# Three row norms of a two-layer kernel: transposed unscaled row by row into one kept tile, scaled and split there

## The chip, the cores and the metric

The kernel is one program on one core of a Trainium2 chip. The metric is the device time of one execution in microseconds. The kernel before was run three times: 2165.43, 2167.75 and 2170.39 us, median 2167.75.

## The reference, cut to what matters

512 tokens of width 1024 go through two transformer layers and a final norm; all data are float32. Every block starts from a row norm, `y = x * rsqrt(mean(x*x) + eps) * gain`, with one factor per token (row) and one gain per column.

```python
# layer 1
h = rms_norm(x, norm_mix);  proj = h @ w_in          # 1024 -> 5632
x = x + (gated mix of a recurrent branch and a differential attention) @ w_out
x = x + hier_moe(rms_norm(x, norm_moe), ...)         # 32 experts, two per token
# layer 2
z = rmsnorm(h, norm_mix_2) @ w_in_2
h = h + (gated mix of an RWKV-7 branch and a sparse attention) @ w_out_2
h = h + cross_attention(rmsnorm(h, norm_cross), rmsnorm(mem, norm_mem), ...)
h = h + hier_moe_2(rmsnorm(h, norm_ffn), ...)
out = rmsnorm(h, norm_final)
```

## The kernel before

The running sum `acc` (128 partitions, four row tiles t of 128 tokens, 1024 columns) stays in SBUF for the whole program. The stages follow one another: `dense1` (layer 1 up to its output projection), `moe` (experts), `dense2` (layer 2 up to its output projection), `cross` (cross attention), `moe` again, `final`. 

**Dense products.** `dense_steps` multiplies normed activations held transposed (`hT`, eight slices k of 128 channels by 512 tokens) with weights. Each operand is held as a high and a low half and a product is three matmuls (`mm3`). For each k a weight slice of 128x512 is split by ACT (`wh`, line 194) and DVE (`wl`, line 195) into three buffers; the split stands in a block of its own with high priority.

**The norm that feeds them** is what the change is about. It stands at three places: at the start of `dense1` (norm_mix), at the start of `dense2` (norm_mix_2) and at the start of `cross` (norm_cross_2). It has three steps. (1) The squares of the rows are summed, in halves of 512 columns as the output projection or the last expert block finishes them (`half_square`, lines 273 to 275; at the start `_norm_tile`, whole rows, row tile by row tile), and `row_scale` (lines 281 to 287) turns them into the four columns of `r`, one factor per token. (2) `_norm4` (lines 289 to 297) multiplies the rows by `r`, three row tiles on DVE and one on ACT, into a tile of 16 KB per partition. (3) `_norm_tp` (lines 299 to 309) turns the scaled rows with 32 transposes on PE into eight PSUM banks, and ACT (line 307, times the gain) and DVE (line 308) split each bank into `hT`'s halves.

**Between the first expert stage and `dense2`** stands a loop (`extra`, line 1075) for expert rows beyond the fixed blocks. It makes no turn with these inputs, but all engines meet at it. The weights of `dense2` are loaded by SP after it.

**Order of the work.** A list scheduler orders each engine's queue from a simulated time line and from priorities: the order of the program, or, inside a block of high priority, a count that starts again at the start of the program. Where `self.pinned` is set (the expert stage), PE's order is the program's. A pool of tiles that is opened over memory of closed pools waits until these are no longer used.

**Weight slots.** Weights of the expert stages come in pieces of 1 MB on SP's queue, in a fixed cycle of slots (`rings`, `plan`, `ahead`, `wslot`): two slots x, seven y, three z, and two m of pool `ringm`, which `moe` opens (line 879). SP issues them in order, each when its slot is free. The same queue loads the weights of `cross`, which go into the slots x and y.

```python
for t, x in enumerate(xs):                               # _norm_tp, lines 303 to 309
    for k, b in enumerate(banks):
        nc.tensor.transpose(b[:, t * 128:(t + 1) * 128], x[:, k * 128:(k + 1) * 128], self.c("ident"))
for k, b in enumerate(banks):
    nc.scalar.activation(hi[:, k, :w], b[:, :w], AF.Copy, scale=gain[:, k:k + 1])
    nc.vector.scalar_tensor_tensor(lo[:, k, :w], b[:, :w], gain[:, k:k + 1], hi[:, k, :w].bitcast(F32),
                                   op0=ALU.mult, op1=ALU.subtract)
```

Of the kernel before, what the change touches and what calls it, by code (L numbers as in the profile page):

```python
# [24 lines left out]
F32 = mybir.dt.float32  # L25
# [4 lines left out]
AF = mybir.ActivationFunctionType  # L30
# [5 lines left out]
D = 1024  # L36
# [141 lines left out]
class Net:  # L178
    def __init__(self, tc, ins, out, at, dump=None):
        self.tc, self.nc, self.I, self.out, self.at = tc, tc.nc, ins, out, at  # L180
        self.dump = dump or {}
        self.es = ExitStack()
        self.pinned, self.late, self.moe_pool = False, None, None
        self.todo, self.ready, self.cur, self.rest, self.bufs = [], [], [], [], {}
        self.banks("a0", "a1", "a2", "a3")
# [33 lines left out]
    def persistent(self):  # L219
        tc, nc, es = self.tc, self.nc, self.es  # L220
        self.P = es.enter_context(tc.tile_pool(name="persist", bufs=1))
        self.ps = es.enter_context(tc.tile_pool(name="ps", bufs=1, space=PSUM))
        P = self.P
        self.acc = P.tile([128, 4, D], F32, name="acc")
        n = sum(v[1] for v in self.at["consts"].values())
        self.cst = P.tile([128, n], F32, name="cst")
        self.dram = es.enter_context(tc.tile_pool(name="dram", bufs=1, space=bass.MemoryType.DRAM))
        self.eps = P.tile([128, 1], F32, name="eps")
        nc.vector.memset(self.eps, 1e-6)
        self.nq = P.tile([128, 3, 4], F32, name="nq")  # L230
        self.r = P.tile([128, 4], F32, name="r")

    def c(self, name):
# [38 lines left out]

    def half_square(self, t, i, junk, vector=False):

        self._square(vector, junk, self.acc[:, t, i * 512:(i + 1) * 512], self.nq[:, i, t:t + 1])

# [11 lines left out]

    def _norm4(self, outs):

        with self.tc.high_priority():
            for t in range(4):
                r = self.r[:, t:t + 1]
                if t == 1:
                    self.nc.scalar.activation(outs[t], self.acc[:, t, :], AF.Copy, scale=r)
                else:
                    self.nc.vector.tensor_scalar(outs[t], self.acc[:, t, :], r, None, op0=ALU.mult)

    def _norm_tp(self, xs, gain, hi, lo):
        nc = self.nc  # L300
        w = len(xs) * 128
        banks = [self.bank(c + str(i)) for c in "da" for i in range(4)]
        for t, x in enumerate(xs):
            for k, b in enumerate(banks):
                nc.tensor.transpose(b[:, t * 128:(t + 1) * 128], x[:, k * 128:(k + 1) * 128], self.c("ident"))
        for k, b in enumerate(banks):
            nc.scalar.activation(hi[:, k, :w], b[:, :w], AF.Copy, scale=gain[:, k:k + 1])
            nc.vector.scalar_tensor_tensor(lo[:, k, :w], b[:, :w], gain[:, k:k + 1], hi[:, k, :w].bitcast(F32),  # L308
                                           op0=ALU.mult, op1=ALU.subtract)

# [22 lines left out]
    def wslot(self, src, pool, tag="wslot", n=None):  # L333

        k = src.shape[1] // 512
        t = pool.tile([128, k, 512], F32, name="wslot", tag=tag, bufs=self.bufs.get((pool, tag)))
# [14 lines left out]
    def ahead(self, n):  # L351
        while self.todo and len(self.ready) < n:
            pool, tag = next(self.where)
            pool = {"late": self.late, "moe": self.moe_pool}.get(pool, pool)
# [61 lines left out]
    def dense1(self, rings, late):  # L416
# [285 lines left out]
        def gate(i):  # L702
            gt[i] = big("gt%d" % i)
            dense(8, hT, "T", lambda j, b: nc.scalar.activation(gt[i][:, j, :], b, AF.Tanh, scale=0.5))
# [168 lines left out]
    def moe(self, W, ring, after=None):  # L873
# [4 lines left out]
        L = es.enter_context(tc.tile_pool(name="moe", bufs=1))  # L878
        self.moe_pool = es.enter_context(tc.tile_pool(name="ringm", bufs=NM))
        acc, cm, br, rs, lps, gain = self.acc, self.cm, self.br, self.rs, self.lps, self.gain  # L880
# [189 lines left out]
        def extra():  # L1070
# [4 lines left out]
            with tc.For_i(0, n):  # L1075
# [28 lines left out]
                for _ in scatter(scat(sid), y, square):  # L1104
                    pass
                self.row_scale()

# [67 lines left out]
        for p in range(16):  # L1175
# [54 lines left out]
        for _ in steps:  # L1230
            pass
        self.pinned = False
        self.row_scale()
# [8 lines left out]
    def dense2(self):  # L1242
# [67 lines left out]
        AR = self.acc.rearrange("p t n -> p (t n)").rearrange("p (q c s n) -> p q c s n", q=4, c=8, s=2)  # L1310
        BK = big("X2", (128, 4, 8, 2, 64))
        v4 = lambda t: t.rearrange("p (c t) -> p c t", t=64)
# [184 lines left out]

        Zs = big("X2", (128, 2, 4, 8, 64))
        Zt, Z = Zs[:, 0], Zs[:, 1]
# [236 lines left out]
        for i in range(2):  # L1736
# [5 lines left out]
            if i == 0:  # L1742
                self.sqrt_table()
        self.row_scale()
        es.close()


    def cross(self, rings, late):
# [13 lines left out]
        hT = [A.tile([128, 8, 512], F32R, name="hT0"), B.tile([128, 8, 512], F32R, name="hT1")]  # L1762
        xn = [x[:, t, :] for x in (B.tile([128, 2, D], F32, name="xn%d" % i, tag="q%d" % i) for i in range(2)) for t in range(2)]
        self._norm4(xn)
        self._norm_tp(xn, col("norm_cross_2"), hT[0], hT[1])
        oT = []
# [73 lines left out]
def net(tc, I, out, at, dump=None):  # L1840
# [3 lines left out]
    def rings(es, n, table, name, first):  # L1844
# [6 lines left out]
        k = len(first)  # L1851
        z, yy, xg, m = ("late", "wslot"), ("late", "yy"), ("late", "xg"), ("moe", "wslot")
        seq = [x] * 2 + [y] * NRING
# [54 lines left out]
```

## Time and profile before

| what | value |
|---|---|
| median of three runs | 2167.75 us (2165.43 to 2170.39) |
| profiled execution, its own time | 2170.49 us |
| its span in the trace | 2168.5 us |
| PE busy | 2079.4 us, 96% of the span |
| first products of `dense1`, `dense2`, `cross` | at 13.66, 1002.35 and 1522.34 us |
| mean granted clock of TensorE | 0.98 of full speed |

Times in the trace are microseconds from the start of the span. A matmul's end is modelled, so PE's busy share says where PE has work, not how fast it goes. Waits are put down to the event that came last.

### The profile page before, as it was taken

Reading aid. Unit: us, or ns where it says so; the run is one execution under the profiler, and the core shown is the slowest. Engines: PE = TensorE matmul, PEld = TensorE weight load, DVE = VectorE, ACT = ScalarE, POOL = GpSimd, SP = SyncE. Lnnn points to the kernel's source line nnn. Section 1 sums busy time; section 2 is a strip of 40 time slices with the busy share of each in tenths; the row PEclk is TensorE's granted clock in tenths of the full one; section 3 lists DMA queues with packets and bytes.
Section 4 is the critical chain, followed back from the end, with each engine's and each line's share of the span. In section 5 each row is a group of like instructions: output and inputs, shape, how many; then the busy total and the mean of one; then the engine's idle time right before and its main releaser. Section 6 shows DMA issues by size and latency. Waiting matters only on the chain. (4 is left out here: it accounts for less than half of the span.)

```text
span 2168.5 us, 29754 instructions
## 1 busy us (share of the span) xinstructions
PE 2079.4 (96%) x11910; PEld 1348.1 (62%) x11914; DVE 986.8 (46%) x2014; ACT 676.4 (31%) x1313; POOL 162.5 (7%) x140
## 2 busy tenths in 40 slices
PE   8999998999999999998988999999998999999996
PEld 6777786785544444546666776767777554444443
DVE  4674344652432333325477474454454332333334
ACT  5364433453111111115434333444444111111112
POOL 0420001200000000000332100011010000000000
PEclk9999999999999999999988999999999999999998
DMA  4222212667999999973122112113532999999994
GB/s 178 87 77 70 75 62 78 247 236 310 412 418 420 419 419 419 419 311 117 61 76 76 40 64 83 54 57 112 228 136 100 375 415 419 420 419 420 419 419 161
DMA packets 96319, 505.87 MB, mean 233 GB/s; under 512 B 21089, under 2 KB 26209, under 8 KB 44465
## 3 DMA queue, kind: packets, MB, share of 16 engines
q1 hardware_dynamic: 90992, 490.09, 56.9%
q10 hardware_dynamic: 4688, 11.66, 1.5%
q0 software_dynamic: 496, 2.17, 0.3%
q8 instruction: 96, 1.57, 0.3%
q14 instruction: 47, 0.38, 0.0%
HBM read 494.83 MB, written 8.91 MB: 232 GB/s over the span
## 5 line engine op out<-in xcount | busy, mean ns | idle before, releaser
L209 PE MATMUL ps_d<-wslot,xg 128*64 128x512 f32 x2048 | 446.4, 592 | 0.0
L209 PE MATMUL ps_d<-hT,wh 128*128 128x512 f32 x1056 | 344.2, 410 | 2.8 <-DVE hT L308 2.8
L209 PEld LDWEIGHTS ps_d<-wslot,xg 128*64 128x64 f32 x2048 | 148.3, 137 | 286.5 <-issue 277.1
L195 DVE TENSOR_TENSOR wl<-wslot,wh 128x512 fp32r<-128x512 f32 x236 | 169.4, 722 | 256.9 <-ACT wh L194 211.0
L194 ACT ACTIVATE wh<-wslot 128x512 fp32r<-128x512 f32 x260 | 163.2, 631 | 310.0 <-PE ps_d L209 239.8
L209 PEld LDWEIGHTS ps_d<-hT,wh 128*128 128x128 f32 x1056 | 197.5, 193 | 54.4 <-issue 9.3
L1023 DVE TENSOR_TENSOR s<-ps_d,s 128x512 f32<-128x512 f32 x32 | 22.1, 692 | 423.0 <-PE ps_d L209 423.0
L209 PE MATMUL ps_d<-hT,wl 128*128 128x512 f32 x528 | 205.7, 402 | 0.0
L209 PE MATMUL ps_a<-wslot,hidT 128*64 128x512 f32 (+1 forms) x832 | 178.3, 578 | 1.7 <-ACT hidT L1031 1.4
L209 PE MATMUL ps_d<-wh,hT 128*128 128x512 f32 x512 | 163.8, 397 | 3.1 <-ACT wh L194 1.4
L1061 DVE TENSOR_TENSOR acc<-acc,ps_a 128x512 f32<-128x512 f32 (+1 forms) x214 | 131.2, 664 | 54.9 <-PE ps_a L209 54.7
L209 PEld LDWEIGHTS ps_a<-wslot,hidT 128*64 128x64 f32 x832 | 58.7, 137 | 108.9 <-issue 100.4
L209 PE MATMUL ps_a<-yy,S 128*128 128x512 f32 (+1 forms) x428 | 114.6, 400 | 5.6 <-DVE acc L1061 5.6
L209 PEld LDWEIGHTS ps_d<-hT,wl 128*128 128x128 f32 x528 | 101.3, 192 | 24.0 <-issue 1.5
L209 PEld LDWEIGHTS ps_d<-wh,hT 128*128 128x128 f32 x512 | 95.6, 188 | 26.9 <-ACT wh L194 1.8
L998 ACT ACTIVATE xg<-ps_a,gain 128x256 f32<-128x256 f32 x102 | 48.2, 475 | 200.0 <-PE ps_a L209 200.0
L209 PE MATMUL ps_a<-oh,xs 128*128 128x256 f32 x816 | 107.1, 285 | 1.4 <-DVE oh L1150 1.4
L209 PEld LDWEIGHTS ps_a<-oh,xs 128*128 128x128 f32 x816 | 100.9, 191 | 9.6 <-issue 9.6
L1049 ACT ACTIVATE yy<-ps_a,gc 128x512 fp32r<-128x512 f32 (+1 forms) x52 | 34.9, 671 | 223.6 <-PE ps_a L209 192.2
L209 PE MATMUL ps_d<-wl,hT 128*128 128x512 f32 x256 | 101.3, 396 | 1.8 <-DVE wl L195 1.8
L209 PEld LDWEIGHTS ps_a<-yy,S 128*128 128x128 f32 x428 | 74.8, 188 | 31.4 <-DVE acc L1061 13.5
L1022 ACT ACTIVATE s<-ps_d 128x512 f32<-128x512 f32 x32 | 19.1, 598 | 199.3 <-PE ps_d L209 199.3
(586 smaller groups left out, 2798.8 us busy)
## 6 DMA issues: line engine op xcount, KB each, us to landing
wslot<-in_wm_dram SPq DMA_DIRECT2D x380, 1024.0 KB, 12.2
wslot<-in_wd_dram SPq DMA_DIRECT2D x108, 512.0 KB, 3.4
wslot<-in_wd_dram SPq DMA_DIRECT2D x19, 1024.0 KB, 15.2
wslot<-in_wm_dram SPq DMA_DIRECT2D x8, 512.0 KB, 14.4
C<-in_x_dram SPq DMA_DIRECT2D x4, 512.0 KB, 5.2
acc<-in_x_dram ACTq DMA_DIRECT2D x4, 512.0 KB, 5.5
kvd<-kvs ACTq DMA_DIRECT2D x8, 256.0 KB, 4.0
xd<-acc ACTq DMA_DIRECT2D x1, 2048.0 KB, 11.1
```

Of the source, the lines that this page charges most:

```text
L194: self.nc.scalar.activation(hi, src, AF.Copy)
L195: (lo_eng or self.nc.vector).tensor_sub(lo, src, hi.bitcast(F32))
L209: self.pin(self.nc.tensor.matmul(*a, **k))
L998: nc.scalar.activation(xg[:, k, :n], b[:, :n], AF.Copy, scale=gain[:, k:k + 1])
L1022: nc.scalar.activation(s1, hb[0], AF.Silu)
L1023: nc.vector.tensor_mul(s1, hb[1], s1)
L1049: nc.scalar.activation(y[0][:, c], b, AF.Copy, scale=gcol)
L1061: nc.vector.tensor_add(acc[:, t, c], acc[:, t, c], b)
```

## The change

The scaling moves behind the transposing. A tile `xt` (8 slices of 128 channels by 512 tokens, 16 KB per partition) is kept for the whole program. As soon as a half row tile of `acc` is final, `turn` transposes its four blocks unscaled into one PSUM bank and copies the bank into `xt`. When `r` is there, `normed` spreads it over partitions with four transposes into one PSUM bank, and for each of the eight slices DVE multiplies `xt` by the gain and by that bank, and `split` (ACT a copy, DVE a subtraction) makes the halves of `hT`. `_norm4` and `_norm_tp` are gone.

At the start of the program the norm by row tiles (`_norm_tile`) gives way to half squares and `turn`s of the loaded rows with one `row_scale` for all. After the first expert stage and in the output projection of `dense2` the `turn`s stand behind the additions to `acc`. The loop's body gets eight `turn`s as well. Squares and copies are divided between ACT and DVE.

`xt` also takes over other tiles: the two slots m (pool `ringm` is gone), the gates `gt0` and `gt1` of `dense1`, and `X2` of `dense2`. The memory reserved at the bottom of SBUF for descriptors of POOL's DMAs goes from its default of 16384 bytes per partition to 4096.

```diff
-    def half_square(self, t, i, junk, vector=False):
-        self._square(vector, junk, self.acc[:, t, i * 512:(i + 1) * 512], self.nq[:, i, t:t + 1])
+    def half_square(self, t, i, junk, vector=False, src=None):
+        src = self.acc[:, t, :] if src is None else src
+        self._square(vector, junk, src[:, i * 512:(i + 1) * 512], self.nq[:, i, t:t + 1])
...
-    def _norm4(self, outs):
-    def _norm_tp(self, xs, gain, hi, lo):
...
+    def turn(self, t, i, tag="a", vector=False, src=None):
+        src = self.acc[:, t, :] if src is None else src
+        b = self.bank(tag, (128, 4, 128))
+        for k in range(4):
+            c = i * 512 + k * 128
+            self.pin(self.nc.tensor.transpose(b[:, k, :], src[:, c:c + 128], self.c("ident")))
+        o = self.xt[:, 4 * i:4 * i + 4, t * 128:(t + 1) * 128]
+        if vector:
+            self.nc.vector.tensor_copy(o, b)
+        else:
+            self.nc.scalar.activation(o, b, AF.Copy)
+
+    def normed(self, gain, hi, lo):
+        nc = self.nc
+        b = self.bank("a")
+        with self.tc.high_priority():
+            for t in range(4):
+                nc.tensor.transpose(b[:, t * 128:(t + 1) * 128], self.r[:, t:t + 1].to_broadcast([128, 128]), self.c("ident"))
+            for k in range(8):
+                x = self.xt[:, k, :]
+                nc.vector.scalar_tensor_tensor(x, x, gain[:, k:k + 1], b, op0=ALU.mult, op1=ALU.mult)
+                self.split(hi[:, k, :], lo[:, k, :], x)
...  wslot
+        if pool == "xt":
+            t = self.xt[:, 4 * self.nxt:4 * self.nxt + 4, :]
+            self.nxt = 1 - self.nxt
...  dense1
-        with tc.high_priority():
-            for t in range(4):
-                self._norm_tile(xin[:, t, :], xin[:, t, :], wk, junk=self.acc[:, t, :])
-        self._norm_tp([xin[:, t, :] for t in range(4)], col("norm_mix"), hT[0], hT[1])
+        for t in range(4):
+            for i in range(2):
+                self.half_square(t, i, self.acc[:, t, i * 512:i * 512 + 512], t % 2, xin[:, t, :])
+                self.turn(t, i, "da"[i] + str(t), t % 2 == 0, xin[:, t, :])
+        self.row_scale()
+        self.normed(col("norm_mix"), hT[0], hT[1])
...  moe, last block of the first stage, behind the addition and square(t, c)
+                    if c.start == 512 and not after:
+                        self.turn(t, 0, "d%d" % (t % 3))
...  moe, behind the last scatter
+        if not after:
+            for t in range(4):
+                self.turn(t, 1, "d%d" % ((t + 1) % 3), t % 2 == 0)
         self.pinned = False
         self.row_scale()
         extra()
...  dense2
-        xn = big("X2", (128, 4, D))
-        self._norm4([xn[:, t, :] for t in range(4)])
-        self._norm_tp([xn[:, t, :] for t in range(4)], col("norm_mix_2"), hT[0], hT[1])
+        self.normed(col("norm_mix_2"), hT[0], hT[1])
...  dense2, output projection, i = 0 and 1
             dense(8, mx, "N", ev_o)
             if i == 0:
                 self.sqrt_table()
+            for t in range(4):
+                self.turn(t, i, vector=i and t % 2)
         self.row_scale()
...  cross
-        self._norm4(xn)
-        self._norm_tp(xn, col("norm_cross_2"), hT[0], hT[1])
+        self.normed(col("norm_cross_2"), hT[0], hT[1])
...  kernel
-    nc = _bacc.Bacc("TRN2", target_bir_lowering=False, num_devices=1)
+    nc = _bacc.Bacc("TRN2", target_bir_lowering=False, num_devices=1, dynamic_dma_scratch_size=4096)
```

## Rows read from the trace of the kernel before

**Rows 1.** The page's part 1: busy us (share of span) xinstructions.

```profile
PE 2079.4 (96%) x11910; PEld 1348.1 (62%) x11914; DVE 986.8 (46%) x2014; ACT 676.4 (31%) x1313; POOL 162.5 (7%) x140
```

**Rows 2.** Waits of PE, whole span: us in total, times, longest.

```profile
PE ps_d L305 <- DVE X L297: 9.7, 1, 9.7
...
PE ps_d L305 <- DVE C L264: 7.1, 1, 7.1
...
PE ps_d L305 <- DVE xn L297: 3.6, 1, 3.6
```

**Rows 3.** Windows, second expert stage; last columns: clock, DMA share, GB/s.

```profile
1740.00:1760.00 20.00, 20.00 (x112) 11.99 (x110) 7.19 (x14) 3.56 (x7) 0.00 (x0) 1.00 1.02 421
```

**Rows 4.** Timeline, start of program: start, us, instructions [idle before, releaser].

```profile
4.58 1.06 ACT L271 ACTIVATE acc<-C 128x1024 f32<-128x1024 f32 x1 [1.40 <-DMA C<-in_x_dram]
...
11.27 0.60 PE L305 MATMUL ps_d<-cst,C 128*128 128x128 f32 x4
...
11.71 0.60 PE L305 MATMUL ps_a<-cst,C 128*128 128x128 f32 x4
...
13.66 0.51 PE L209 MATMUL ps_d<-wh,hT 128*128 128x512 f32 x1 [1.36 <-DVE hT L308]
```

**Rows 5.** Timeline, from the first expert stage to dense2.

```profile
988.51 0.69 DVE L269 SCALAR_TENSOR_TENSOR sq<-acc 128x512 f32<-128x512 f32 x1 [1.36 <-ACT sq L271]
...
989.77 0.18 DVE L287 RECIPROCAL r<-nq 128x4 f32<-128x4 f32 x1 [0.36 <-ACT nq L286]
...
991.65 1.15 ACT L295 ACTIVATE X<-acc,r 128x1024 f32<-128x1024 f32 x1 [1.91 <-DVEq L1075]
...
991.94 25.77 SPq L338 DMA_DIRECT2D wslot<-in_wd_dram  x6
...
995.74 1.12 PE L305 MATMUL ps_d<-cst,X 128*128 128x128 f32 x4 [9.70 <-DVE X L297]
...
995.98 0.63 ACT L194 ACTIVATE wh<-wslot 128x512 fp32r<-128x512 f32 x1 [3.18 <-DMA wslot<-in_wd_dram]
...
1002.35 0.73 PE L209 MATMUL ps_d<-hT,wh 128*128 128x512 f32 x2 [0.80 <-DVE hT L308]
```

**Rows 6.** Windows of 1 us, same place; third from end: granted clock.

```profile
990.00:991.00 1.00, 0.00 (x0) 0.00 (x0) 0.00 (x0) 0.00 (x0) 0.00 (x0) 0.50 0.00 0
...
1001.00:1002.00 1.00, 0.55 (x6) 0.31 (x3) 0.46 (x1) 1.00 (x3) 0.00 (x0) 1.00 1.03 442
```

**Rows 7.** Groups by line, 960 to 1004 us: count, busy us, mean ns.

```profile
L271 ACT ACTIVATE sq<-acc 128x512 f32<-128x512 f32 x14 | 8.8, 630 | 14.3 <-PE ps_d L1029 12.2 <-DVE acc L1061 1.8
...
L195 DVE TENSOR_TENSOR wl<-wslot,wh 128x512 fp32r<-128x512 f32 x3 | 2.0, 690 | 0.7 <-ACT wh L194 0.7
...
L271 ACT ACTIVATION_READ_ACCUMULATOR sq<-acc 128x1 f32 x14 | 2.6, 186 | 0.0
...
L308 DVE SCALAR_TENSOR_TENSOR hT<-ps_d,cols,hT 128x512 fp32r<-128x512 f32 x4 | 2.7, 745 | 1.1 <-ACT hT L307 1.1
```

**Rows 8.** Line 1031, ACT's copies from PSUM: ns min/median/max.

```profile
L1031 ACT ACTIVATE hidT<-ps_d x32: 582/600/600, 525.8 to 2138.4; 128x512 f32<-128x512 f32 x32
```

**Rows 9.** Timeline, from dense2 to cross.

```profile
1491.32 1.32 PE L209 MATMUL ps_d<-wh,hT 128*128 128x512 f32 x5
...
1509.45 0.40 PE L209 MATMUL ps_d<-wh,hT 128*128 128x512 f32 x1
...
1511.65 4.26 SPq L338 DMA_DIRECT2D wslot<-in_wd_dram  x8
...
1512.18 0.18 DVE L287 RECIPROCAL r<-nq 128x4 f32<-128x4 f32 x1 [0.36 <-ACT nq L286]
...
1518.69 1.67 ACT L194 ACTIVATE wh<-wslot 128x512 fp32r<-128x512 f32 x3 [1.39 <-DMA wslot<-in_wd_dram]
...
1522.34 1.22 PE L209 MATMUL ps_d<-hT,wh 128*128 128x512 f32 x2 [2.04 <-DVE hT L308]
```

**Rows 10.** Waits of SP's queue, 1500 to 1520 us.

```profile
SPq L338 <- ACT k L271: 0.9, 1, 0.9
```

More of the change, by code (lines that the diff above doesn't have):

```diff
@@ L182, in __init__ @@
         self.es = ExitStack()
-        self.pinned, self.late, self.moe_pool = False, None, None
+        self.pinned, self.late = False, None
         self.todo, self.ready, self.cur, self.rest, self.bufs = [], [], [], [], {}
@@ L231, in persistent @@
         self.r = P.tile([128, 4], F32, name="r")
+        self.xt = P.tile([128, 8, 512], F32, name="xt")
+        self.nxt = 0
     def c(self, name):
@@ L287, in row_scale @@
             nc.vector.reciprocal(self.r, nq[:, 2, :])
-    def _norm4(self, outs):
+    def turn(self, t, i, tag="a", vector=False, src=None):
[12 more added lines that the diff above has]
+        b = self.bank("a")
         with self.tc.high_priority():
             for t in range(4):
[L293 to L297, printed above, removed]
-    def _norm_tp(self, xs, gain, hi, lo):
[L300 to L309, printed above, removed]
+                nc.tensor.transpose(b[:, t * 128:(t + 1) * 128], self.r[:, t:t + 1].to_broadcast([128, 128]), self.c("ident"))
[3 more added lines that the diff above has]
+                self.split(hi[:, k, :], lo[:, k, :], x)
     def tok_sums(self, b, sq, c, ind):
@@ L335, in wslot @@
         k = src.shape[1] // 512
-        t = pool.tile([128, k, 512], F32, name="wslot", tag=tag, bufs=self.bufs.get((pool, tag)))
+        if pool == "xt":
+            t = self.xt[:, 4 * self.nxt:4 * self.nxt + 4, :]
+            self.nxt = 1 - self.nxt
+        else:
+            t = pool.tile([128, k, 512], F32, name="wslot", tag=tag, bufs=self.bufs.get((pool, tag)))
         src = src.rearrange("p (k n) -> p k n", k=k)
@@ L353, in ahead @@
             pool, tag = next(self.where)
-            pool = {"late": self.late, "moe": self.moe_pool}.get(pool, pool)
+            pool = self.late if pool == "late" else pool
             src, c = self.todo.pop(0)
@@ L702, in gate @@
         def gate(i):
-            gt[i] = big("gt%d" % i)
+            gt[i] = big("gt%d" % i) if i > 1 else self.xt[:, 4 * i:4 * i + 4, :]
             dense(8, hT, "T", lambda j, b: nc.scalar.activation(gt[i][:, j, :], b, AF.Tanh, scale=0.5))
@@ L878, in moe @@
         L = es.enter_context(tc.tile_pool(name="moe", bufs=1))
-        self.moe_pool = es.enter_context(tc.tile_pool(name="ringm", bufs=NM))
         acc, cm, br, rs, lps, gain = self.acc, self.cm, self.br, self.rs, self.lps, self.gain
@@ L1105, in extra @@
                     pass
+                if not after:
+                    for t in range(8):
+                        self.turn(t % 4, t // 4, "d%d" % (t % 3))
                 self.row_scale()
@@ L1231, in moe @@
             pass
+        if not after:
+            for t in range(4):
+                self.turn(t, 1, "d%d" % ((t + 1) % 3), t % 2 == 0)
         self.pinned = False
@@ L1310, in dense2 @@
         AR = self.acc.rearrange("p t n -> p (t n)").rearrange("p (q c s n) -> p q c s n", q=4, c=8, s=2)
-        BK = big("X2", (128, 4, 8, 2, 64))
+        BK = self.xt.rearrange("p a b -> p (a b)").rearrange("p (q c s n) -> p q c s n", q=4, c=8, s=2)
         v4 = lambda t: t.rearrange("p (c t) -> p c t", t=64)
@@ L1496, in select @@
                 nc.vector.tensor_scalar(bias[:, bo[i]:bo[i] + n], sc[:, :n], -2.0e38, NEG, op0=ALU.is_gt, op1=ALU.mult)
-        Zs = big("X2", (128, 2, 4, 8, 64))
+        Zs = self.xt.rearrange("p a b -> p (a b)").rearrange("p (x m h n) -> p x m h n", x=2, m=4, h=8)
         Zt, Z = Zs[:, 0], Zs[:, 1]
@@ L1762, in cross @@
         hT = [A.tile([128, 8, 512], F32R, name="hT0"), B.tile([128, 8, 512], F32R, name="hT1")]
-        xn = [x[:, t, :] for x in (B.tile([128, 2, D], F32, name="xn%d" % i, tag="q%d" % i) for i in range(2)) for t in range(2)]
-        self._norm4(xn)
-        self._norm_tp(xn, col("norm_cross_2"), hT[0], hT[1])
+        self.normed(col("norm_cross_2"), hT[0], hT[1])
         oT = []
@@ L1851, in rings @@
         k = len(first)
-        z, yy, xg, m = ("late", "wslot"), ("late", "yy"), ("late", "xg"), ("moe", "wslot")
+        z, yy, xg, m = ("late", "wslot"), ("late", "yy"), ("late", "xg"), ("xt", None)
         seq = [x] * 2 + [y] * NRING
```

## The prediction

> **What bounds the kernel now.** I read the page's busy shares first: PE has work for 96% of the span [rows 1], so only a place where PE stands idle, or has less to do, can give much. The list of PE's waits names such places, and three of its four longest belong to the transposes of the three norms, line 305: 9.7 us at the start of `dense2`, 7.1 us at the start of the program, 3.6 us at the start of `cross` [rows 2]. The windows of the expert stages show another bound: the DMA engines are busy throughout at 421 GB/s [rows 3]. There an earlier start carries through to the end, and a slot that is free earlier does not. Then I read the timeline at each of the three places for the chain that ends at the first dense product.
>
> At the start, row 0 is there at 4.58 and the first product runs at 13.66 [rows 4]. Before `dense2`, the last squares end with a DVE square that had waited 1.36 us for ACT's squares, `r` is ready at 989.95, the loop's meeting releases ACT at 991.65 and SP at 991.94, the transposes start at 995.74 and the first product at 1002.35 [rows 5]. Before `cross`, the last product ends at 1509.85, `r` at 1512.36, and the first product starts at 1522.34 [rows 9].
>
> In all three the old chain is: `r`, scaled rows, 32 transposes, split, product. The new one is: `r`, four transposes, one multiplication, split, product. What matters is which other condition ends last then.
>
> **Second norm (`dense2`).** New chain behind the meeting: four transposes at the low clock 1.12 [rows 5], a multiplication 0.75 [rows 7], ACT's copy 0.63: 991.65 + 2.5 = 994.2. But the weights are later: SP asks for the first at 991.94, ACT splits it from 995.98 to 996.61 [rows 5]. So 996.6 is the floor, 5.7 us before 1002.35, and the norm's 16 DVE operations then run beside the product. Against it stands a later meeting. The `turn`s put 32 transposes and eight copies ahead of it; PE and DVE have room, but ACT's squares are what the last DVE square waited for [rows 5], and ACT gets four copies among them (first halves; 0.60 each [rows 8]): 2.4 us. The two later ACT copies and DVE's two fall beside the last square and the root. Bounds for this delay: none if they find ACT's gaps, 6 x 0.60 + 2 x 0.69 = 5.0 if all stand ahead of `r` (DVE's by another pass over 128x512 [rows 7, 8]). I take 2.4: the row with the wait says that ACT's order sets `r`. First product: 999.0, 3.3 us earlier.
>
> From this the clock takes back a part. During PE's wait the granted clock is at 0.50 (1.2 GHz), and with nothing but transposes on PE from 995.74 it is at 1.00 (2.4 GHz) in the window from 1001 [rows 5, 6]. So in the kernel before the transposes spend the slow time, some 4.3 us; in the new one PE waits for weights, and the products spend it, losing half: 2.1 us. Gain of this place: 3.3 - 2.1 = **1.2 us**, bounds 5.7 (no delay, no slow time) and 5.7 - 5.0 - 2.1 = -1.4.
>
> The Trainium skill, page "TensorE: Matmul & The Clock Gate", section "Part 4: PE-mode transpose", says that transposes do not count as PE activity for the full clock. By that, the products at 1002.35 would have been slow before as well, the 2.1 us would be no new cost, and this place would give 3.3. Rows 6 disagree, and I go by them.
>
> **Third norm (`cross`).** The first halves' 16 transposes move into the output projection, which PE bounds: a group of four goes by in 11.71 - 11.27 = 0.44 us at full clock [rows 4], four groups 1.8 us; the last product ends at 1511.65. `r` came 2.5 us behind it [rows 9]; now ACT also has three weight splits, 1.67 [rows 9], if the weights are there, and one copy, 0.60 [rows 8], ahead of the root: 1516.4. Then 1.12 + 0.75 + 0.63: first product at 1518.9, **3.4 us** earlier.
>
> Are the weights there? Before, they were asked for at 1511.65 and split from 1518.69, 7.0 us later [rows 9], because the pool of the first slots lay over the work pool of `dense2`: the wait was for the last square's scratch [rows 10]. Counting tile sizes in the code, the change frees 12 KB at the top of `dense2` (reserve 12 KB less, `X2` 16 KB gone, `xt` 16 KB added below), so the two slots x (16 KB behind 3 KB of router tiles) lie over free memory and the two-slot ring of `dense2`, which is done some us before the end. SP can then ask earlier, if the scheduler puts these loads ahead of the key and value loads, which wait for PE's last product. If not, they shift with the squares: 1511.65 + 1.8 + 7.0 + 0.63 = 1521.1, a gain of 1.2. Upper bound: splits and copy behind the root, 1516.6, a gain of 5.7. I take the early ones, as loads are ordered by when they can start. The slow clock is paid at the first products in both (two took 1.22 us at 1522.34 against 0.73 at 1002.35 [rows 5, 9]).
>
> **First norm (start).** Here nothing covers, and row by row becomes all rows at once. ACT, from 4.58: four half squares of 0.63 + 0.19 [rows 7], four copies of 0.60 [rows 8], three weight splits 1.67 (as in [rows 9]): 7.4, to 12.0. Root and reciprocal 0.5 (as the 0.36 and 0.18 in [rows 5]), four transposes 0.60 [rows 4], multiplication 0.75, split 0.63: 14.5. The low half comes 0.69 later [rows 7], of which two matmuls hide about 0.4: 14.8, so **1.1 us lost**. Bounds: 0.5 gained if the weight splits go behind, 3.2 lost if DVE's three low halves of weights (2.1) stand between `r` and the multiplication.
>
> **At nothing.** The multiplications and subtractions of the later slices: 0.745 + 0.690 a slice and 0.690 for a weight's low half [rows 7], 2.1 us on DVE, against 12 matmuls of PE: five in a row take 1.32 with one's 0.40 as the tail, so 0.23 each and 2.8 in all [rows 9]. If that cover went, see the third rival. Slots m in `xt`, the gates, `X2`'s other uses: same traffic, and in the expert stages the full DMA hides it [rows 3]; slots free earlier could bring 2 MB forward, 5.0 us at 421 GB/s, but SP's queue stops at the next used slot. The smaller reserve touches POOL's few loads, which are needed a whole dense product later; no row shows it.
>
> **Sum.** 1.2 + 3.4 - 1.1 = 3.5 us less than the profiled execution's 2170.49, which stands 2.74 above the median. From the median: 2167.75 - 3.5 = **2164.3 us**. 0.2% is 4.3 us, about what a measurement of this kernel can tell from no change.
>
> **Rivals.**
> *The copies vanish and the clock holds.* If ACT's gaps take the copies and PE's shorter waits keep the clock up, second and third norm give their upper bounds: 5.7 + 5.7 - 1.1 = 10.3, 2157.5 us. For it: ACT is busy for 31% only [rows 1]. Against: the weights' floor leaves PE waiting. Chance 0.26.
> *The weights stay late in `cross`.* 1.2 + 1.2 - 1.1 = 1.3, 2166.5 us. For it: the queue had put the key and value loads first. Chance 0.15.
> *DVE does its whole norm first* (slower). If the 16 operations of `normed` go ahead of the weights' low halves on DVE, the third matmul waits for 8 x 1.435 = 11.5 and 0.69. It decides where the first low half stands behind the last multiplication. First products: 12.5 + 0.6 + 12.2 = 25.3; 991.65 + 2.4 + 1.1 + 12.2 = 1007.3; 1516.4 + 1.1 + 12.2 = 1529.7; together 24 us later, 2191.8 us. For it: both stand in blocks of high priority, and `_norm_tp` did not. Against: each block counts from its own start, so a low half, second in its block, ranks ahead of a multiplication, fifth or later. Chance 0.11.
> *The kept tile ties its two slots.* If a load into one m waited for the readers of the other, each of 13 rounds would drain the ring: hundreds of us. Against: `acc` is already written in one slice while another is read. Chance 0.01.
> *The products were slow before as well.* The low clock at the first products of `dense2` in both kernels: 3.5 + 2.1 = 5.6, 2162.1 us. The windows speak against it [rows 6]. That is the Trainium skill's rule above. Chance 0.03.
>
> **How the numbers follow.** The forecast keeps 0.44: 0.17 of it beyond 4.3 us of gain, 0.25 within 0.2%, 0.02 slower. Faster: 0.17 + 0.26 + 0.03 = 0.46; same: 0.25 + 0.15 = 0.40; slower: 0.02 + 0.11 + 0.01 = 0.14. All upper bounds together give 11.9 us, 2155.9; all lower bounds -3.2 - 1.4 + 1.2 = -3.4, 2171.1. The range is 2156 to 2171; outside it lie the third and fourth rival.
>
> **What would show it.** Right: no scaled rows; first products near 14.8, 999 and 1519; PE idle before `dense2` ended by the weights; the meeting some 2 us later; a clock of 0.50 at the first products of `dense2`; the weights of `cross` asked for ahead of the key and value loads. Wrong: weights' low halves late on DVE, a meeting as early as before or 5 us later, SP asking for the first weights behind `dense2`'s last product, or PE's gain given back within the next product.

## The result, and the profile after

The changed kernel takes 2183.64 us (median of five, 2178.61 to 2184.42), against 2167.88 us of the kernel before beside it: ratio 1.0063, 95% interval 1.0047 to 1.0078. That is 15.8 us slower by the medians and 13.7 by the ratio. The forecast was 2164.3, the range ended at 2171. The profiled execution took 2184.42 us, its span is 2182.6, its mean clock 0.976.

The page's part 1 hardly moves against [rows 1]: PE has 7 us more to do in a span that is 14 us longer.

```profile
PE 2086.7 (96%) x11938; PEld 1351.5 (62%) x11942; DVE 996.7 (46%) x2042; ACT 678.6 (31%) x1328; POOL 161.2 (7%) x140
```

The waits of PE (total, times, longest) say more. The three on line 305 [rows 2] are gone; in their place PE waits for the constants (line 298, 4.8 us at the start), for `r` and the meeting (line 311, the spreading), then for ACT's high half, and then, three times, for a low half `hT` from DVE.

```profile
PE ps_a L311 <- DVE r L290: 7.1, 2, 3.9
PE ps_d L209 <- ACT hT L194: 6.7, 2, 5.1
...
PE ps_d L209 <- DVE hT L195: 5.2, 3, 2.5
...
PE ps_a L311 <- DVEq L1086: 4.7, 1, 4.7
```

The timeline shows the same picture at all three places. DVE makes the eight multiplications (line 314) in one go, and the first low half (line 195) only behind the last. In order, start of the program, `dense2` and `cross`:

```profile
13.68 5.36 DVE L314 SCALAR_TENSOR_TENSOR xt<-xt,cols,ps_a 128x512 f32<-128x512 f32 x8 [0.23 <-PE ps_a L311]
14.53 0.63 ACT L194 ACTIVATE hT<-xt 128x512 fp32r<-128x512 f32 x1 [0.82 <-DVE xt L314]
15.22 0.80 PE L209 MATMUL ps_d<-wh,hT 128*128 128x512 f32 x1 [1.57 <-ACT hT L194]
18.96 0.69 DVE L195 TENSOR_TENSOR hT<-xt,hT 128x512 fp32r<-128x512 f32 x1
19.70 2.50 PE L209 MATMUL ps_d<-wh,hT 128*128 128x512 f32 x5 [0.70 <-DVE hT L195]
24.83 1.32 PE L209 MATMUL ps_d<-wh,hT 128*128 128x512 f32 x5
...
999.95 0.69 DVE L271 SCALAR_TENSOR_TENSOR sq<-acc 128x512 f32<-128x512 f32 x1 [1.32 <-ACT sq L273]
1001.21 0.18 DVE L290 RECIPROCAL r<-nq 128x4 f32<-128x4 f32 x1 [0.36 <-ACT nq L289]
...
1004.20 1.95 DVE L1476 CAST X<-cst 128x128 bf16<-128x128 f32 x1 [2.81 <-issue]
1004.24 1.82 POOL L1408 MEMSET qT<- 128x2048 f32 x1
1006.28 5.22 DVE L314 SCALAR_TENSOR_TENSOR xt<-xt,cols,ps_a 128x512 f32<-128x512 f32 x8
1007.91 0.63 ACT L194 ACTIVATE wh<-wslot 128x512 fp32r<-128x512 f32 x1 [6.73 <-DMA wslot<-in_wd_dram]
1008.96 1.13 ACT L194 ACTIVATE hT<-xt 128x512 fp32r<-128x512 f32 x2
1009.63 2.08 PE L209 MATMUL ps_d<-hT,wh 128*128 128x512 f32 x4 [5.13 <-ACT hT L194]
1011.58 0.68 DVE L195 TENSOR_TENSOR wl<-wslot,wh 128x512 fp32r<-128x512 f32 x1
1013.00 1.28 DVE L195 TENSOR_TENSOR hT<-xt,hT 128x512 fp32r<-128x512 f32 x2
1013.73 0.79 PE L209 MATMUL ps_d<-hT,wh 128*128 128x512 f32 x1 [2.03 <-DVE hT L195]
1014.32 0.63 PE L209 MATMUL ps_d<-hT,wl 128*128 128x512 f32 x1
...
1496.63 19.96 SPq L348 DMA_DIRECT2D wslot<-in_wd_dram  x4
...
1521.67 0.39 PE L209 MATMUL ps_d<-wh,hT 128*128 128x512 f32 x1
1522.13 0.80 SPq L1790 DMA_DIRECT2D kv<-kvd  x2
1525.95 1.32 ACT L194 ACTIVATE kv<-kv 128x256 fp32r<-128x256 f32 x4
1527.50 0.18 DVE L290 RECIPROCAL r<-nq 128x4 f32<-128x4 f32 x1 [1.35 <-ACT nq L289]
1528.89 5.36 DVE L314 SCALAR_TENSOR_TENSOR xt<-xt,cols,ps_a 128x512 f32<-128x512 f32 x8 [1.21 <-PE ps_a L311]
1530.40 2.04 PE L209 MATMUL ps_d<-hT,wh 128*128 128x512 f32 x4 [1.55 <-POOL kv L195]
1534.16 4.89 DVE L195 TENSOR_TENSOR hT<-xt,hT 128x512 fp32r<-128x512 f32 x8
1534.90 0.80 PE L209 MATMUL ps_d<-hT,wh 128*128 128x512 f32 x1 [2.46 <-DVE hT L195]
```

Read the matmuls' own times beside the waits. A product of this size shows 0.63 us alone at the low clock and five in a row 2.50; from 24.83 on five take 1.32, as at full clock [rows 9]. In the kernel before, the first two of `dense2` took 0.73 together [rows 5]; here four take 2.08. The windows say it directly (third from the end is the granted clock): 0.50, that is 1.2 GHz, while the first products of `dense2` run and 6 us later still.

```profile
1009.00:1010.00 1.00, 0.37 (x1) 0.37 (x2) 1.00 (x2) 1.00 (x3) 0.00 (x0) 0.50 1.17 471
1015.00:1016.00 1.00, 1.00 (x3) 0.74 (x3) 1.00 (x2) 0.00 (x0) 0.00 (x0) 0.50 1.06 371
```

**A ledger by place.** I paired each matmul of a profile with the same one (line, tiles, count) of the profile before and took the median difference of their starts over 20 us. It is positive where the kernel is later. "Start" is the lateness at 40 us; "second" is what is added from 940 to 1040 us (last expert blocks, meeting, first products of `dense2`); "third" what is added from 1460 to 1560 us (output projection, first products of `cross`). These columns come from one execution of each kernel, and not always a middling one: that of order + filler is the fastest of twelve (2159.81 us), that of order + filler + own the slowest (2171.55). The medians are those of all runs of a kernel; the ratios are against the kernel before beside it on the same chip, and differences between kernels of different groups are better read from them (0.001 is 2.2 us). All rows but the first are the experiments told below; "own" is the edit of the last expert block.

```
kernel                              median   ratio (95%)              start second third
changed                             2183.64  1.0063 (1.0047, 1.0078)   5.8    4.2   2.0
order                               2172.57  1.0012 (1.0001, 1.0023)   3.1    1.5  -1.7
old start                           2181.31  1.0052 (1.0036, 1.0068)   0.0    4.2   1.9
old second norm                     2175.33  1.0034 (1.0021, 1.0047)   3.7   -0.6   1.1
memory alone                        2171.06  1.0008 (0.9995, 1.0020)   0.1   -0.6  -0.4
order + turns behind the meeting    2171.43  1.0018 (1.0007, 1.0029)   4.9    0.7  -1.0
... + old start                     2170.32  1.0005 (0.9989, 1.0020)   0.1    1.8  -1.2
... + other use of the kept tile    2172.53  1.0022 (1.0009, 1.0036)   0.8    1.9  -2.7
order + filler                      2162.93  0.9974 (0.9963, 0.9985)   2.1   -0.2  -4.0
before + filler                     2165.97  0.9980 (0.9968, 0.9991)   0.9    0.1  -2.3
order + filler, old start, own      2167.20  0.9994 (0.9980, 1.0007)   0.7   -1.0  -4.0
third norm alone, order + filler    2169.32  0.9996 (0.9987, 1.0004)   0.0    0.7  -3.8
order + filler + own                2164.08  0.9978 (0.9967, 0.9989)   1.4    1.5  -4.0
changed + filler                    2179.41  1.0049 (1.0033, 1.0065)   4.0    5.1   0.8
```

### The profile page after: what moved, and what is told of

Same layout as the page of the kernel before. It is cut to its first block, busy times and chain, and to the rows that moved or that the text cites. A ratio compares the mean times of both kernels' runs of the same rounds, so it can differ in the third digit from the quotient of the medians.

```text
span 2182.6 us, 29856 instructions
## 1 busy us (share of the span) xinstructions
PE 2086.7 (96%) x11938; PEld 1351.5 (62%) x11942; DVE 996.7 (46%) x2042; ACT 678.6 (31%) x1328; POOL 161.2 (7%) x140
## 5 line engine op out<-in xcount | busy, mean ns | idle before, releaser
L209 PE MATMUL ps_d<-wslot,xg 128*64 128x512 f32 x1744 | 415.9, 592 | 0.0
L209 PE MATMUL ps_d<-hT,wh 128*128 128x512 f32 x1056 | 348.9, 413 | 11.2 <-ACT hT L194 5.1
L209 PEld LDWEIGHTS ps_d<-wslot,xg 128*64 128x64 f32 x1744 | 136.5, 137 | 244.4 <-issue 235.0
L209 PE MATMUL ps_a<-wslot,hidT 128*64 128x512 f32 (+1 forms) x744 | 171.3, 576 | 1.7 <-ACT hidT L1042 1.4
L209 PE MATMUL ps_d<-xt,xg 128*64 128x512 f32 x304 | 103.3, 593 | 0.0
## 6 DMA issues: line engine op xcount, KB each, us to landing
xt<-in_wm_dram SPq DMA_DIRECT2D x54, 1024.0 KB, 11.1
```

What stands on the lines that cost most here:

```text
L209: self.pin(self.nc.tensor.matmul(*a, **k))
```

## The experiments

**The order on DVE** (label e1_order). In `normed`:

```diff
+            lows = []
             for k in range(8):
                 x = self.xt[:, k, :]
-                nc.vector.scalar_tensor_tensor(x, x, gain[:, k:k + 1], b, op0=ALU.mult, op1=ALU.mult)
-                self.split(hi[:, k, :], lo[:, k, :], x)
+                with self.tc.issue_after(lows[k - 2]) if k >= 2 else ExitStack():
+                    nc.vector.scalar_tensor_tensor(x, x, gain[:, k:k + 1], b, op0=ALU.mult, op1=ALU.mult)
+                nc.scalar.activation(hi[:, k, :], x, AF.Copy)
+                lows.append(nc.vector.tensor_sub(lo[:, k, :], x, hi[:, k, :].bitcast(F32)).ins)
```

> The changed kernel with one edit: in all three norms the multiplication of slice k is queued on DVE behind the low half of slice k-2, so the first low half follows the second multiplication and not the eighth. Theory (DVE's order): the waits of PE for a low half (0.70 us at the start, 2.03 before dense2, 2.46 before cross) go, and the half-clocked stretch behind them starts earlier; together 5 to 8 us less than the changed kernel, about 2177. Rival (the clock): the price lies in the products at 1.2 GHz, which start as cold as before; the waits only change places and less than 2 us come back, 2182 or more. Rival (the turns): what costs is ahead of the reciprocal and stays, so the reciprocal before dense2 is again some 11 us later than in the kernel before, under both.

2172.57 us: 11.1 us come back, more than the 5 to 8 expected; the three places of the ledger hold 9.1 of them. The waits for a low half of `hT` are gone from the head of PE's list, and the multiplications and low halves alternate; the timeline of this run before `dense2` and `cross`:

```profile
1004.06 1.27 DVE L316 SCALAR_TENSOR_TENSOR xt<-xt,cols,ps_a 128x512 f32<-128x512 f32 x2
...
1007.34 0.69 DVE L318 TENSOR_TENSOR hT<-xt,hT 128x512 fp32r<-128x512 f32 x1
1007.95 0.74 DVE L316 SCALAR_TENSOR_TENSOR xt<-xt,cols,ps_a 128x512 f32<-128x512 f32 x1
...
1007.36 2.50 PE L209 MATMUL ps_d<-hT,wh 128*128 128x512 f32 x5 [5.05 <-ACT hT L317]
...
1522.17 2.47 PE L209 MATMUL ps_d<-hT,wh 128*128 128x512 f32 x5 [1.55 <-POOL kv L195]
```

The order was the largest single loss. Part of what is left is visible in the last two rows: five products in 2.50 us, still at the low clock.

**Filler against the clock** (label e9_warm, and e14_filler_alone without the order). Transposes of the identity into an unused bank, ahead of and behind the spreading of the factors, where PE is idle:

```diff
-            for t in range(4):
-                nc.tensor.transpose(b[:, t * 128:(t + 1) * 128], self.r[:, t:t + 1]...
+            for n in range(pre + 4 + post):
...
+                    i = nc.tensor.transpose(junk[:, 0:128], self.c("ident"), self.c("ident"))
+                if n or pre:
+                    self.tc.keep_in_program_order(i)
```

> The kernel of the order run with filler: 20 and 8, 0 and 16, 30 and 10 transposes of the identity into an unused bank, ahead of and behind the spreading of the factors, at the start, before dense2 and before cross; PE is idle there otherwise. Theory (the clock follows PE's own idle time): the first eight to twelve products of each place take 0.23 us each and not 0.43; 1.8 + 2.4 + 2.4 = 6.6 us less than the order run, 2166. Rival (only products count, transposes do not): the products are as slow as before and the time stays at 2172 or rises by the filler that PE has not finished when the first half is there.

> The changed kernel with the filler of the filler run, but all eight multiplications still ahead of the low halves on DVE. Theory (the low halves first): PE starts its first products at full clock, has them done sooner and then waits longer for the low half, so at most the half-clock stretch behind that wait comes back at each place; 2 to 5 us less than the changed kernel, 2179 to 2182. Rival (the clock is everything, the waits only let it fall): as much as in the order run, 9.6 us, about 2174 or less.

With the order, 2162.93: 9.6 us less than without filler (8.2 by the ratios), and faster than the kernel before (0.9974). The first products of `dense2` now show the full clock at once, five in 1.43, behind 16 fillers; those of `cross` take 1.78 (the copies of keys and values by POOL release the first), and there too the granted clock is 1.00:

```profile
996.77 3.62 PE L315 MATMUL ps_d<-cst 128*128 128x128 f32 x16
1002.00 1.43 PE L209 MATMUL ps_d<-hT,wh 128*128 128x512 f32 x5 [1.62 <-ACT hT L323]
...
1512.77 1.78 PE L209 MATMUL ps_d<-hT,wh 128*128 128x512 f32 x5 [0.46 <-POOL kv L195]
```

Without the order the filler gives only 4.2 us (2179.41; 3.0 by the ratios), as the first theory said, and the intervals of the two ratios overlap. The first four products run at full clock, and PE then waits longer for the low half than in the changed kernel (before `dense2` 2.93 against 2.03, before `cross` 3.33 against 2.46). Before `dense2` the clock falls again in that wait, in `cross` right behind it (0.68 in the window from 1531, 0.50 in the next); at the start, with a wait of 2.37, it does not:

```profile
1006.78 1.20 PE L209 MATMUL ps_d<-hT,wh 128*128 128x512 f32 x4 [0.96 <-ACT hT L194]
1010.90 0.79 PE L209 MATMUL ps_d<-hT,wh 128*128 128x512 f32 x1 [2.93 <-DVE hT L195]
1011.50 0.63 PE L209 MATMUL ps_d<-hT,wl 128*128 128x512 f32 x1
...
1530.78 0.51 PE L209 MATMUL ps_d<-hT,wh 128*128 128x512 f32 x1 [3.33 <-DVE hT L195]
```

By the ratios order alone gives 11, filler alone 3, both 19 us; each ratio is uncertain by some 3 us either way, so that both together give more than their sum is not shown by the times. The rows show how the two losses hang together: a late operand leaves PE idle, and the products behind it can run at the low clock.

**Filler in the kernel before** (label e10_before_filler): 22, 14 and 30 transposes of the identity ahead of the 32 of `_norm_tp`.

> The kernel before, norms unchanged, with filler (transposes of the identity into the first bank) ahead of the 32 transposes: 22 at the start, 14 before dense2, 30 before cross. Theory (the filler pays where first products were slow): in this kernel only cross began its products at 1.2 GHz, so some 2 us come back there and nothing at the other two places, 2166. Rival (filler helps wherever PE would be idle, through the stretches behind it as well): as much as it gave to the order run, 2160 or less, and the changed norms would have no part in that gain.

2165.97, as the first theory said: 3.1 us (4.3 by the ratio), of which the ledger places 2.3 in `cross`, the one place where this kernel began its products at the low clock [rows 9]. The changed norms with order and filler stand at 0.9974 and this at 0.9980; the intervals overlap, so that the new norms add to the filler's gain is not shown.

**One norm at a time** (labels e2_start_old, e3_second_old, e5_memory). The norm of one place as before, or all three.

> The changed kernel with the norm at the start as before (row tile by row tile, scaled rows, 32 transposes); the other two norms and the memory are the changed ones. Theory (three places): the first product of dense1 is back at 13.7 at full clock; the 6 us that dense1 runs late at 40 us are gone and stay gone through the expert stage, 2178 us or less. Rival (the expert stage absorbs it): the first expert stage is bounded by its transfers, which do not start earlier, so the reciprocal before dense2 comes no earlier and the time stays at 2183.

> The changed kernel with the second norm (before dense2) as before: scaled rows in the kept tile, 32 transposes, no turns in the last expert block. Theory (three places): the last block gets back 1.7 us, the reciprocal 1.6, and the products of dense2 run at full clock from the start: dense2 settles 4.2 us earlier, 2179.4 us. Rival (the wait for the weights is what counts): the first weights of dense2 come no earlier against the meeting, so only the earlier meeting counts, 3.3 us, 2180.3; if the time stays above 2182 the place costs nothing and the loss sits in the start.

> The changed kernel with all three norms as before: what is left of the change is the memory (the kept tile, slots m, gates and X2 in it, the smaller reserve at the bottom). Theory (the norms are all of it): within 2 us of the kernel before, ratio 0.999 to 1.001. Rival (the memory): the two slots m in the kept tile are taken by the gates until dense1 is through, so the first expert weights come later and the transfers' share from 450 to 500 us stays at 0.50 and not 0.64; 2 to 4 us slower than before, ratio 1.001 to 1.002.

The old start gives back 2.3 us (2181.31) where 5.6 were expected: the start is 5.8 us late at 40 us in the changed kernel and 0.0 here, but the expert stage begins only 3.2 us earlier (4.9 us late against 8.1). The gain shrank in one stretch where nothing was edited: from 320 to 340 us the granted clock is 0.80 in this execution and 1.00 in that of the changed kernel, and the lateness goes from 0.0 to 3.8. The execution of the memory run does the same (0.79, from 0.1 to 3.8). The old second norm gives 8.3 us (2175.33; 6.3 by the ratios), where its place shows 4.8 (from 4.2 to -0.6). The memory alone is 1.0008 (0.9995 to 1.0020): no difference that can be told, so the norms are nearly all of the loss, though the rival's 1.001 to 1.002 is not excluded. Its sign is there: the transfers' share from 450 to 500 us is 0.48, against 0.64 in the kernel before. And in `dense1` SP's second load into the kept tile is issued when the gate's last reader is through, the ten loads of the output projection stand behind it, and PE waits 3.17 us for a weight (1.38 in the kernel before):

```profile
405.63 0.33 SPq L370 DMA_DIRECT2D xt<-in_wm_dram  x1
407.38 16.51 SPq L370 DMA_DIRECT2D wslot<-in_wd_dram  x10
...
415.25 1.20 PE L209 MATMUL ps_d<-wh,hT 128*128 128x512 f32 x4 [3.17 <-ACT wh L194]
```

**Turns behind the meeting, old start, other use of the tile** (labels e6_behind, e7_behind_start, e8_slots), each on top of the one before. The first takes the `turn`s out of the last expert block and into `normed` of `dense2`, and keeps the first three weight splits on ACT behind the first halves' copies; the third is

```diff
-        dv = big("dv")
+        dv = self.xt[:, 4:8, :]
...
-            gt[i] = big("gt%d" % i) if i > 1 else self.xt[:, 4 * i:4 * i + 4, :]
+            gt[i] = big("gt%d" % i) if i else self.xt[:, 0:4, :]
```

> The kernel of the order run (low half of slice k-2 ahead of the multiplication of slice k), with the second norm's transposes and copies taken out of the last expert block and put behind the meeting, where PE waits for the first weights of dense2. Theory (the turns delay the meeting, and the wait for the weights is free): the last scatter and the reciprocal stand against the kernel before as the expert stage does (some 5.9 us late and no more), the transposes keep PE busy in the wait, so the first products run at full clock, and dense2 settles at 2 to 4 us against the kernel before, where the order run has 7.4; 3.5 to 5.5 us less than the order run, about 2168. Rival (the chain behind the meeting is longer): copies on ACT and multiplications beside POOL's memset put the first product no earlier than in the order run, dense2 settles at 6.5 or more, 2171.5 or more.

> The same with the norm at the start as in the kernel before. Theory: dense1 runs 2 to 3 us earlier, of which 1 reaches the first expert stage, as the run with the old start alone showed (4.9 us late there and not 5.9); 1 us less than the run before this one, about 2167. Rival: the entry of the expert stage is set by something else by now, no difference between these two.

> The same, and the second half of the kept tile holds in dense1 the values of the attention (dv, dead by 320 us) in place of the second gate, which goes back to a tile of its own. Theory (SP's queue): the second load into the kept tile no longer waits for the last reader of the gate, the ten weight loads behind it on SP's queue come 1.8 us earlier against PE, and PE's 3.2 us wait at the output projection of dense1 shrinks to some 1.4; the expert stage starts 1.8 us earlier, about 2165. Rival (the clock): the late entry is a matter of the granted clock between 330 and 340 us and the order of the loads changes nothing.

2171.43, 2170.32 and 2172.53: the first and the last were misses, and of the second only the difference came, about 1 us, not the level. The turns did delay the meeting: without them the reciprocal comes at 994.64, 4.87 us after the kernel before, as the stage (4.9 late), where the changed kernel's came 11.4 late with the stage 8.1 late. But the chain behind the meeting stayed long. The fourth copy ends at 1001.83, the multiplications wait for it, and ACT's first high half stands behind a weight split that waits for its DMA and two more copies; the first product is at 1006.43:

```profile
994.64 0.18 DVE L290 RECIPROCAL r<-nq 128x4 f32<-128x4 f32 x1 [0.36 <-ACT nq L289]
...
1001.23 0.60 ACT L303 ACTIVATE xt<-ps_d 128x512 f32<-128x512 f32 x1 [0.93 <-PE ps_d L298]
1003.64 0.63 ACT L194 ACTIVATE wh<-wslot 128x512 fp32r<-128x512 f32 x1 [0.78 <-DMA wslot<-in_wd_dram]
1005.76 1.14 ACT L321 ACTIVATE hT<-xt 128x512 fp32r<-128x512 f32 x2
1006.43 1.42 PE L209 MATMUL ps_d<-hT,wh 128*128 128x512 f32 x5 [3.41 <-ACT hT L321]
```

`dense2` settles at 5.6, between the two theories (2 to 4, 6.5 or more). The other use of the tile did what its theory said in its place, SP's loads at 399.90 and not 407.53, PE's wait 1.44 and not 2.47, yet the time did not follow: its profile lost 1.5 us between 80 and 85 us, at a granted clock of 0.50 from 82 to 84, as those of two later kernels did that keep `dv` where it was.

**Adding the parts** (labels e11_best, e12_third_alone, e13_own_scatter). The second edit of the first, alone in the third, lets `turn` and the squares run in the last expert block for its own scatter only:

```diff
-            def done(t, c):
-                if last:
-                    if t == c.start == 0 and after:
-                        after(xgs())
+            def done(t, c, mine=last):
+                if last and t == c.start == 0 and after:
+                    after(xgs())
+                if mine:
```

> The filler run with the norm at the start as in the kernel before, and in the last expert block turns and squares for that block's own scatter alone (in the kernel before and the changed one they run for the scatter of the block ahead of it as well). Theory (the parts add up): the last scatter no longer falls behind by 2.3 us between 960 and 990 us, of which 1.7 reach dense2; the start gives 1 us at the expert stage; 2.7 us less than the filler run, about 2160. Rival (the squares set the reciprocal, not PE): no difference to the filler run, 2163.

> The kernel with the first and second norm as before and the third one as in the filler run (order, filler of 30 and 10). Theory (the gain sits in cross): the ledger of the filler run gives 5.8 us between the last product of dense2 and the products of cross, less 1.8 us for the 16 transposes in the output projection, so 4 us less than the run with the memory alone (2171.1), about 2167; the filler run's further 4 us come from the other two places. Rival (the first two places are worth nothing): 2163, as the filler run.

> The filler run with one more edit: in the last expert block turns and squares run for that block's own scatter alone. Theory (the start made the last run miss): dense2 settles 0.8 us earlier than in the filler run, as in the run with the old start and this edit, and the time is 2162, at or just below the filler run. Rival (this edit costs, for instance since ACT and PE reach the meeting in another order): 2165 or more, and the old start is not to blame.

2167.20 was a miss: 4.3 us above the filler run where 2.7 below were expected. The own-scatter edit alone gives 2164.08, like the filler run, and its profile loses more in the second place, not less (1.5 against -0.2). That would make the old start the worse partner, though its place costs less (0.7 against 2.1). It is not shown: the intervals of the two runs overlap (0.9980 to 1.0007, 0.9967 to 0.9989), and the twelve executions with the old start fall into two groups, five from 2162.52 to 2163.54 at a mean clock of 0.985 or more and seven from 2167.02 to 2172.83 at 0.984 or less. The third norm alone gives 2169.32, 1.7 below the memory run (2.6 by the ratios) where 4 were expected and its place shows 3.4 (-3.8 against -0.4). In its place the third norm with order and filler is worth the same in all four kernels that have it: -4.0, -4.0, -3.8, -4.0.

## Why the prediction was wrong

**The step that failed** is the one titled "At nothing". It counted DVE's work per slice (2.1 us against PE's 2.8), which is right, and took for granted that DVE does it slice by slice. The queue had all eight multiplications first, 5.2 to 5.4 us in one go, and no low half of `hT` before they were done. The cover was there in sum and absent at the time it was needed. The order run shows the price: 11.1 us.

**The third rival came nearest to the mechanism**, with a chance of 0.11. It had all 16 operations (11.5 us) ahead of the first weight's low half. It was the eight multiplications, and what came late at all three places was the norm's own low half. The sign that it named was there before `dense2` alone, where the first weight's low half starts at 1011.58, behind the last multiplication. Its 24 us became 12.0 in the three places of the ledger. Its reason against, that a low half ranks ahead of a fifth multiplication by its priority, did not hold, and why is not shown: at the start ACT's first high half ends at 15.16, with five multiplications still to start, and they go ahead all the same. The order is fixed before the run, from the scheduler's simulated times, which no run shows.

**The first products** came nearly where the sum had them. At the start 15.22 against 14.8. Before `dense2` 0.8 us earlier than before, measured against the stage (1009.63 - 8.1 against 1002.35), where 3.3 were forecast. Some 1.1 us of the difference is ACT's order: the first weight split ends at 1008.54, where the sum had the product, but ACT splits a second weight and only then makes the high half. Before `cross` the span from the last product to the first one is 8.7 us (1521.67 to 1530.40) against 12.9 [rows 9]: 4.2 earlier, forecast 3.4. Together 3.4 us earlier, forecast 5.6 before the clock's part. I costed the way to the first product with care and the second to twelfth with a glance; that is where most of it went. One reading was wrong, though no number hangs on it: of PE's four longest waits two, not three, belong to the transposes; the 3.6 us of `cross` come behind waits of 4.4 and 4.2 elsewhere.

**The meeting** comes 3.3 us later against the stage (11.4 - 8.1), forecast 2.4. ACT's copies are in it, as said. Not foreseen: `done` runs for the scatter of the block ahead as well, so there were turns twice; the last scatter is 9.8 us late already where the stage is 8.1. But repairing this alone gained nothing that the runs can tell (2164.08 against 2162.93).

**The clock** was forecast at 0.50 for the first products of `dense2`, at a cost of 2.1 us. It was so there, in `cross` as in the kernel before, and, not foreseen, at the start, and the products paid for longer, since PE stopped again for a low half at each place. So this term was too small, and that is most of why the order alone does not reach the forecast. The three places of the order run add up to 2.9 us lost, where 3.5 gained were forecast; with the filler they add up to 2.1 gained. The filler thus restores 5.0 of the 6.4 us there, in one execution of each. On the Trainium skill's rule (page "TensorE: Matmul & The Clock Gate", section "Part 4: PE-mode transpose") that transposes do not bring the full clock, the trace disagrees a second time: PE ran nothing but transposes ahead of 1002.00 in the filler run, and the products stand at full clock behind them (five in 1.43 us).

**Right:** no scaled rows; the weights of `cross` asked for ahead of keys and values (SP loads weights from 1496.63 and comes to keys and values at 1522.13; three weights are split between the squares, from 1522.21). In `cross` four splits of keys went ahead of the root too (1525.95), which was not counted. **The slots** at nothing: nearly, by the ratio (1.0008, no difference that can be told); in their place 1.8 us of wait, of the kind the step itself named, a queue that stops at a slot still in use.

**Not settled.** Order + filler, with or without the own-scatter edit, lies 5 to 6 us below the kernel before, while its three places hold some 2 and 1. The rest arises where nothing was edited. The granted clock differs there (below), and what sets it was not found.

## What to carry to other kernels

Where a norm is cut into slices, it is not enough that an engine has time for all of it: write out its queue and pin the order that the consumer needs. An earlier first product is worth nothing if PE then stops for the second operand, and a stop can cost twice, once as a wait and once as products at the low clock. Where PE must wait ahead of a product, cheap transposes in the wait paid for themselves in the order run and in the kernel before; where the second operand was late too, their gain is not clear of the noise. Of a sum of 3 us in a kernel of 2168, judge by the place in the trace and by many runs: one profile moves by more than that elsewhere.

## What the runs showed of the hardware

**The same code, another clock.** The filler run and the one with the own-scatter edit have the same `dense1`. In the one the clock held until 341 us, in the other it fell at 333, and the same matmuls took nearly twice as long. First the timeline of the filler run, then that of the other:

```profile
333.73 1.16 PE L701 MATMUL ps_a<-k,F 128*128 128x128 f32 x8 [0.26 <-DVE onr L713]
...
335.90 2.00 PE L705 MATMUL ps_a<-E,hgS 128*128 128x64 f32 x16
```

```profile
333.12 1.82 PE L701 MATMUL ps_a<-k,F 128*128 128x128 f32 x8 [0.26 <-DVE onr L713]
...
336.87 3.67 PE L705 MATMUL ps_a<-E,hgS 128*128 128x64 f32 x16
```

The expert stage then begins 0.1 us early in the first and 5.6 late in the second. Executions of one kernel scatter with the clock as well: those of the memory run go from 2164.01 us at a mean clock of 0.984 to 2177.98 at 0.978. An estimate from these figures: 0.006 of 2170 us is 13.0 us, the distance is 14.0. What lets the clock fall in one execution and not in the other is not shown.

**DVE beside POOL.** Behind the meeting a CAST of 128x128 on DVE took 1.95 us, as long as POOL's MEMSET beside it (1.82); it held the first multiplication to 1006.28. In the kernel before, the same CAST came behind the MEMSETs and took 0.22. There the three scalings stood beside them (POOL's MEMSET of `qT` ran from 993.26 to 995.08) and took 4.26 us, where one takes 0.75 at the start. So some 2 us of the wait for scaled rows that the change removed were such a stop:

```profile
992.75 4.26 DVE L297 TENSOR_SCALAR X<-acc,r 128x1024 f32<-128x1024 f32 x3 [2.80 <-issue]
...
996.93 0.22 DVE L1459 CAST X<-cst 128x128 bf16<-128x128 f32 x1
```

The Trainium skill (page "SBUF — State Buffer", section "Who interferes with whom") says that a cast on DVE can take ports that it shares with POOL, and that one of the two then stands still for the whole instruction of the other. The trace agrees: the CAST ends as the MEMSET does, at 1006.1; which of the two came first cannot be read, their starts are 0.04 us apart.
